# A hybrid decoder layer on one core: which memory the first tiles of the last phase take, and how the final norm is shared out

## The chip, the cores and the metric

The kernel runs on 1 core of a Trainium2 chip. The metric is the device time of one execution in microseconds (us), and the median of several runs stands for a kernel. A core has a matrix engine (PE, whose weight loads are listed as PEld), a vector engine (DVE), a scalar engine (ACT), a general engine (POOL, GpSimd) and a sync engine (SP). Each works through its own list of instructions in order. They meet through semaphores and the on-chip memory (SBUF); matrix products arrive in a separate accumulation memory (PSUM). Transfers are issued from SP, ACT or GpSimd.

## The reference, cut to what matters

One decoder layer over 512 tokens of width 2048: four token mixers side by side, a projection, cross-attention to a memory, and a squared-ReLU MLP of width 8192, with a final RMSNorm. The change lies in the MLP's second half and the norm.

```python
    hn = rmsnorm(h, norm_mlp_g[l])
    h = h + jnp.einsum('blf,fd->bld', jnp.square(jax.nn.relu(jnp.einsum('bld,df->blf', hn, w_up[l]))), w_down[l])
return rmsnorm(h, norm_final_g)
# y = x * rsqrt(mean(x * x) + 1e-6) * g
```

Arithmetic is float32. Every product is made of three matmuls in a reduced format: a value is split into a high part (an ACT copy) and a low part (a DVE subtraction), and high*high, high*low and low*high are added.

## The kernel before

**Phases.** Up to about 799 us come the mixers, the projection and the cross-attention. The up phase (799 to 1494 us) computes the MLP's hidden values in 8 chunks `q` of 4 calls `up_pair(q, pr)`. Each call makes two row blocks by `gemm`, whose weight units go through `wload` (L120 loads 512 KB into `wr`, L125 is the ACT copy `wh`, L126 the DVE difference `wl`). It then squares them, forms seven sums and differences in `z`, splits them into `zh` (L146) and `zl` (L147), and GpSimd stores both to DRAM tensors `ud[q, 0]` and `ud[q, 1]` (L984). The residual goes to DRAM as `xd` tiles. The down phase, from about 1495 us, multiplies the hidden values with `w_down`.

**The down phase.** It is a Strassen-like scheme: a chunk has seven products in place of eight. `down_chunk(q)` loads four blocks of `w_down`: `b22` (1,1), `b11` (0,0), `b12` = (0,1) + (0,0), and `b21` (1,0). A sum of two blocks in memory is made by a second, accumulating load from GpSimd (L1098 with `accum_op`). The products come in the order idx 6, 0, 4, 5, 3, 2, 1; here product 0 is the first, idx 6. Each has its `u` tiles (two DMAs of 512 KB from `ud`, L1026), for some a combination of raw weights on DVE (L1045), four splits of raw weights (L1047 on ACT gives `w2h`, L1048 on DVE gives `w2l`; a ring of five pairs), 48 matmuls (L1057 to L1059) into four PSUM banks, and four evictions into one or two of the accumulators `x1` to `x7` (L1066 the first time on ACT, else L1068 on DVE). `merge` adds accumulators in the last chunks.

**The tail.** In the last chunk, products idx 3 and idx 2 finish the token half `t = 1` (`x7`, `x4`) and the upper columns of `t = 0` (`x3`); idx 1 finishes `x2`. `tail_sums` squares finished tiles on ACT with a row sum, `tail_rs` adds the sums and takes the inverse square root by eleven small DVE operations (`rsqrt`: L161, L162, then three rounds of L166 to L168), and `tail_out` scales a row block by the inverse root and the weight in one DVE operation of 1024 columns (L1170) and stores it from SP (L1173). For `x3`, DVE multiplies by the weight ahead of time (L1132), and ACT scales (L1183).

**Memory and order.** Tiles live in pools, and a pool that is opened after another was closed reuses its memory, each new tile waiting for the old tiles under it. `home` (L998) names the pool of each tile of the down phase: `p2a`, over the residual tiles that are free before the up phase is; `p2x`, over the first half of the activations; `p2w`, over the weight buffers of `wload`; and all others in `p2`, over the second half of the activations and the up phase's `z`, `zh`, `zl`. The order of instructions on an engine is set by a planner, before the run. In its own simulated time it takes, at each moment, the ready instruction of highest priority. Priority is program order, and `urgent()` lifts what is inside it ahead of all that isn't lifted. So an urgent load can go out long before its place in the program, as soon as its memory is free in the planner's view.

Of the kernel before, what the change touches and what calls it, by code (L numbers as in the profile page):

```python
# [13 lines left out]
I32 = mybir.dt.int32  # L14
# [42 lines left out]
def trunk(ctx, tc, A, out):  # L57
# [7 lines left out]
    def pool(name, bufs=1, **kw):  # L65
        return ctx.enter_context(tc.tile_pool(name=name, bufs=bufs, **kw))
# [917 lines left out]
                G.dma_start(ud[q, i][:, :, pr], t.bitcast(F32))  # L984

    NC_ = DFF // P // FC
    for q in range(NC_):
        for pr in range(4):
            up_pair(q, pr)


    zc.close()
    wa.close()
    p2w = pool("down_w", side="left", reuse_waits="tile")
    p2x = pool("down_x", side="left", reuse_waits="tile")
    p2 = pool("down", side="left", reuse_waits="tile")
    acc = {}
# [4 lines left out]
    def slot(name, shape, dt):  # L1002
        return home.get(name, p2).tile(shape, dt, name=name)

    def acc_tile(i):
        t = slot(f"x{i}", [P, 2, 2, L], F32)
# [5 lines left out]
    def flat(t):  # L1012
        return t.rearrange("p a n -> p (a n)")

    us, ws = [0], [0]

    def raw2(n):
        return [slot(f"wq{n}{j}", [P, 4, L], F32) for j in range(2)]

    def u_load(q, idx):  # L1020
        n = us[0] % 3
        us[0] += 1
        uu = []
        for i in range(2):
            t = slot(f"u{n}{i}", [P, 4, 256], F32R)
            Q.dma_start(t.bitcast(F32), ud[q, i][:, idx])  # L1026
            uu.append(t)
        return uu

    def w_tiles():  # L1030
        n = ws[0] % 5
        ws[0] += 1
# [1 line left out]

    sets = [True]

    def down_product(q, idx, w, comb, acc_to, last=None):
        with urgent():
            uu = u_load(q, idx)
# [30 lines left out]
        if last:  # L1070
            for b in range(2):
                for j in range(2):
                    part(j, 0, b)
                    part(j, 1, b)
                    evict(j, b)
                last(b)
# [13 lines left out]

    def down_chunk(q):
        last = q == NC_ - 1
        b22, b11, b12, b21 = (raw2(n) for n in ((0, 1, 2, 3), (1, 2, 0, 3), (2, 0, 1, 3))[q % 3])

        def load(b, i, k, eng=Q, **kw):
            with urgent():
                for j in range(2):
                    eng.dma_start(b[j], A["w_down"][q, i, k, :, j], **kw)  # L1098
# [5 lines left out]
        if not q:  # L1104
# [5 lines left out]
        load(b21, 1, 0)  # L1110
        if q == NC_ - 3:
            merge(2, 2, 1, OP.add)
            merge(6, 6, 1, OP.add)
# [4 lines left out]
        down_product(q, 4, b22, (OP.add, b22, b22, b12), (6,))  # L1118
# [4 lines left out]
        down_product(q, 5, b11, (OP.subtract, b11, b22, b11), (-7, 4) if last else (7,))  # L1123
        load(b22, 1, 0, G, accum_op=OP.add)
        down_product(q, 3, b12, (), (3, 7) if last else (5,))
        if last:
            tail_sums(1, 1, 7)
            tail_sums(0, 1, 3)
            with urgent():
                for b in range(2):  # L1130
                    x = flat(acc[3][:, b])
                    V.tensor_tensor(x, x, fin["g"][:, 1024:], op=OP.mult)  # L1132
# [4 lines left out]
        down_product(q, 2, b22, (), (4,))  # L1137
        if last:
            tail_sums(1, 0, 4)
            tail_rs(slice(2, 4))  # L1140
            with urgent():
                for b in range(2):
                    tail_out(1, b, 1, 7)
                    tail_out(1, b, 0, 4)
        down_product(q, 1, b21, (), (2,), tail if last else None)

    ssq = cp.tile([P, 4, 4], F32, name="sx")
    rf = cp.tile([P, 4], F32, name="rf")
    ss1 = cp.tile([P, 4], F32, name="ss1")
    G.memset(ssq.rearrange("p a b -> p (a b)"), 0.0)  # L1150
    fin = {}

    def tail_sums(t, i, a):
        if not fin:
            g, sq = raw2(NC_ % 3)
            fin["g"], fin["sq"] = flat(g), flat(sq)
            Q.dma_start(fin["g"], A["fin_row"].to_broadcast([P, D]))
        with urgent():
            for b in range(2):
                S.activation(fin["sq"][:, :1024], flat(acc[a][:, b]), AF.Square,  # L1160
                             accum_out=ssq[:, 2 * t + b, i:i + 1])

    def tail_rs(sl):
        with urgent():
            V.reduce_sum(ss1[:, sl], ssq[:, sl], axis=AX.X)
            rsqrt(rf[:, sl], ss1[:, sl], 1.0 / D, EPS)

    def tail_out(t, b, i, a):
        x = flat(acc[a][:, b])
        V.scalar_tensor_tensor(x, x, rf[:, 2 * t + b:2 * t + b + 1], fin["g"][:, 1024 * i:1024 * i + 1024],  # L1170
                               op0=OP.mult, op1=OP.mult)
        r0 = 256 * t + P * b
        Q.dma_start(out[r0:r0 + P, 1024 * i:1024 * i + 1024], x)  # L1173

    def tail(b):
        with urgent():
            for j in range(2):
                S.activation(fin["sq"][:, 1024:1024 + L], acc[2][:, b, j], AF.Square,
                             accum_out=ssq[:, b, 2 * j:2 * j + 1])
            tail_rs(slice(b, b + 1))  # L1180
            tail_out(0, b, 0, 2)
            x = flat(acc[3][:, b])
            S.activation(x, x, AF.Copy, scale=rf[:, b:b + 1])  # L1183
            Q.dma_start(out[P * b:P * b + P, 1024:], x)

    for q in range(NC_):
        down_chunk(q)
# [86 lines left out]
```

## Time and profile before

| | |
|---|---|
| median of 3 runs | 2160.16 us (2156.77 to 2161.19) |
| the profiled execution | 2154.79 us, its span 2152.4 us |
| PE busy | 2088.5 us, 97% of the span |
| DVE, ACT, POOL busy | 1479.9, 907.7, 109.3 us |
| chain that ended last | PE 82%, DVE 7%, DMA 5% |

The span is the time from the first to the last event of the profile; the execution's own time is a little longer. A window row gives, for a stretch of the span, the busy time of each engine and, in brackets, how many instructions that was. The clock is the granted clock of PE as a share of the full one. In a timeline a row gives start, duration, engine, line and operation, with the idle time ahead of it and what ended that in square brackets.

### The profile page before, as it was taken

The page shows a single profiled execution, that of the slowest core. Times are in us where ns is not written, and L with a number is a line of the kernel's source. Part 1 is how long each engine was busy: PE and PEld are TensorE (multiplying, and loading weights), DVE is VectorE, ACT ScalarE, POOL GpSimd, SP SyncE. Part 2 cuts the span into 40 slices and gives each one's busy share as a digit, 9 for nine tenths or more (in the row PEclk, how much of TensorE's full clock was granted, in tenths as well). Part 3 has the DMA queues.
Part 4 walks back from the last instruction along what each step waited for, and adds up shares of the span by engine and source line. Part 5 has one row for each costly group of instructions (what it writes and reads, how often), then busy time and mean ns, then how long its engine had stood idle before and what let it go on. Part 6 is the DMA issues. An engine that isn't in the chain of part 4 may idle for free.

```text
span 2152.4 us, 24931 instructions
## 1 busy us (share of the span) xinstructions
PE 2088.5 (97%) x9340; PEld 1699.7 (79%) x9340; DVE 1479.9 (69%) x2143; ACT 907.7 (42%) x1229; POOL 109.3 (5%) x166
## 2 busy tenths in 40 slices
PE   8999999999999999899999999999699999999997
PEld 6777778777988788688888888888588888888885
DVE  7999999996767663544444444445376777887898
ACT  7565552557434553333233333333343333333334
POOL 0000000100000000100000000000000000000000
PEclk9999999999999999999999999999899999999998
DMA  8553325533433136765655555555879769778872
GB/s 304 169 173 115 116 82 181 164 111 107 143 98 113 40 126 252 254 199 167 197 168 193 167 195 170 188 179 186 298 246 288 253 212 321 233 226 300 250 238 98
DMA packets 111527, 404.83 MB, mean 188 GB/s; under 512 B 13088, under 2 KB 14752, under 8 KB 98992
## 3 DMA queue, kind: packets, MB, share of 16 engines
q1 hardware_dynamic: 89232, 303.64, 41.0%
q0 software_dynamic: 22176, 99.62, 16.5%
q8 instruction: 73, 1.20, 0.2%
q14 instruction: 46, 0.38, 0.1%
HBM read 326.64 MB, written 76.04 MB: 187 GB/s over the span
## 4 chain that ended last, share of the span: by engine, by line
PE 82%; DVE 7%; DMA 5%; issue 2%; ACT 2%; SPq 0%; POOL 0%; ACTq 0%; DVEq 0%; POOLq 0%
PE mm L130 17%; PE mm L132 17%; PE mm L131 16%; PE mm L1058 4%; PE mm L1059 4%; PE mm L1057 4%; PE two L1057 2%; PE two L1058 2%; PE sm L1058 2%; PE sm L1057 2%; PE two L1059 2%; PE sm L1059 2%; DVE wl L126 2%; PE acc L1058 1%; PE acc L1057 1%
## 5 line engine op out<-in xcount | busy, mean ns | idle before, releaser
L132 PE MATMUL mm<-ah,wl 128*128 128x512 f32 (+1 forms) x1920 | 742.9, 387 | 8.3 <-DVE wl L126 8.3
L130 PE MATMUL mm<-ah,wh 128*128 128x512 f32 (+1 forms) x1920 | 743.8, 387 | 5.5 <-ACT wh L125 3.4
L131 PE MATMUL mm<-al,wh 128*128 128x512 f32 (+1 forms) x1920 | 740.2, 385 | 0.0
L125 ACT ACTIVATE wh<-wr 128x1024 fp32r<-128x1024 f32 (+1 forms) x296 | 275.6, 932 | 582.6 <-PE mm L131 450.5
L126 DVE TENSOR_TENSOR wl<-wr,wh 128x1024 fp32r<-128x1024 f32 (+1 forms) x296 | 314.6, 1064 | 182.2 <-ACT wh L125 180.0
L132 PEld LDWEIGHTS mm<-ah,wl 128*128 128x128 f32 x1920 | 361.5, 188 | 84.8 <-DVE wl L126 11.1
L130 PEld LDWEIGHTS mm<-ah,wh 128*128 128x128 f32 x1920 | 361.4, 188 | 82.2 <-ACT wh L125 5.2
L131 PEld LDWEIGHTS mm<-al,wh 128*128 128x128 f32 x1920 | 361.5, 188 | 73.7 <-issue 4.3
L1047 ACT ACTIVATE w2h<-wq 128x1024 fp32r<-128x1024 f32 x224 | 237.6, 1061 | 385.4 <-PE two L1059 106.3
L1048 DVE TENSOR_TENSOR w2l<-wq,w2h 128x1024 fp32r<-128x1024 f32 x224 | 271.1, 1224 | 135.7 <-ACT w2h L1047 135.5
L973 DVE SCALAR_TENSOR_TENSOR r<-mm,rsx 128x512 f32<-128x512 f32 x64 | 44.2, 691 | 165.8 <-PE mm L132 165.0
L1058 PE MATMUL mm<-w2l,u 128*128 128x512 f32 x336 | 132.2, 394 | 0.5 <-DVE w2l L1048 0.5
L1057 PE MATMUL mm<-w2h,u 128*128 128x512 f32 x336 | 131.1, 393 | 1.6 <-ACT w2h L1047 1.6
L1059 PE MATMUL mm<-w2h,u 128*128 128x512 f32 x336 | 132.1, 393 | 0.0
L147 DVE TENSOR_TENSOR zl<-z,zh 128x1792 fp32r<-128x1792 f32 x32 | 64.8, 2026 | 58.4 <-ACT zh L146 50.9
L1057 PE MATMUL two<-w2h,u 128*128 128x512 f32 x224 | 88.5, 396 | 16.9 <-DMA u<-ud 16.9
L1045 DVE TENSOR_TENSOR wq<-wq,wq 128x1024 f32<-128x1024 f32 x64 | 77.7, 1223 | 16.9 <-DMA wq<-in_w_down 16.7
L1058 PE MATMUL two<-w2l,u 128*128 128x512 f32 x224 | 88.5, 395 | 0.0
L1058 PE MATMUL sm<-w2l,u 128*128 128x512 f32 x224 | 88.4, 395 | 0.0
L1057 PE MATMUL sm<-w2h,u 128*128 128x512 f32 x224 | 88.2, 394 | 0.0
L1059 PE MATMUL two<-w2h,u 128*128 128x512 f32 x224 | 87.9, 393 | 0.0
L1059 PE MATMUL sm<-w2h,u 128*128 128x512 f32 x224 | 87.9, 393 | 0.0
(362 smaller groups left out, 2419.3 us busy)
## 6 DMA issues: line engine op xcount, KB each, us to landing
wr<-in_w_up SPq DMA_DIRECT2D x128, 512.0 KB, 3.6
wq<-in_w_down SPq DMA_DIRECT2D x64, 1024.0 KB, 7.8
u<-ud SPq DMA_DIRECT2D x112, 512.0 KB, 6.0
wq<-in_w_down POOLq DMA_DIRECT2D x32, 1024.0 KB, 12.2
wr<-in_w_in SPq DMA_DIRECT2D x56, 512.0 KB, 3.9
ud<-zh POOLq DMA_DIRECT2D x32, 896.0 KB, 4.7
ud<-zl POOLq DMA_DIRECT2D x32, 896.0 KB, 8.1
wr<-in_w_out SPq DMA_DIRECT2D x64, 256.0 KB, 2.9
```

The source lines that it names most:

```text
L125: S.activation(h, r, AF.Copy)
L126: V.tensor_tensor(l, r, h.bitcast(F32), op=OP.subtract)
L130: T.matmul(o, wh, xh, start=start, stop=False)
L131: T.matmul(o, wh, xl, start=False, stop=False)
L132: T.matmul(o, wl, xh, start=False, stop=stop)
L147: V.tensor_tensor(l, src, h.bitcast(F32), op=OP.subtract)
L1045: V.tensor_tensor(flat(r[1]), flat(r[2]), flat(r[3]), op=comb[0])
L1047: S.activation(flat(h), flat(r[0]), AF.Copy)
L1048: V.tensor_tensor(flat(l), flat(r[0]), flat(h).bitcast(F32), op=OP.subtract)
L1057: T.matmul(o[2 * j + b], uh, h[:, p], start=a == 0 and p == 0, stop=False)
L1058: T.matmul(o[2 * j + b], uh, l[:, p], start=False, stop=False)
L1059: T.matmul(o[2 * j + b], ul, h[:, p], start=False, stop=a == 1 and p == 1)
```

## The change

In chunk 0, `b22` and `b11` now are the raw tiles `wq0` and `wq1`, both in the early pool, and their loads and the first `u` load are written into the up loop behind the pairs (1,0), (1,2), (2,0), (2,2) and (3,0). `b12` of chunk 0 takes `wq2`, over the first half of the activations; it is loaded with (0,1), and (0,0) is added by four DVE operations from `b11` and no longer by an accumulating load. The third `u` pair moves from `p2` to the pool over the weight buffers; `wq3` (`b21`) with `x1` and `x6` gets a pool of its own over the second half of the activations; `x7`, `x4`, `x2`, `x5` lie over the old `z`, `zh`, `zl`. In the tail, sums and norms are taken per row block; the inverse root is reached by eight DVE operations after the last square, where it was a sum and eleven; GpSimd multiplies `x7`, `x3` and half of the last blocks by the weight; ACT and DVE share the scalings; and ACT issues half of the stores.

```diff
+    home = {n: "a" for n in ("wq00", "wq01", "wq10", "wq11", "u00", "u01", "w2h0", "w2l0", "w2h1", "w2l1")}
+    home.update({n: "x" for n in ("wq20", "wq21", "u10", "u11", "w2h2", "w2l2")})
+    home.update({n: "w" for n in ("w2h3", "w2l3", "w2h4", "w2l4", "x3", "u20", "u21")})
+    home.update({n: "b" for n in ("wq30", "wq31", "x1", "x6")})
...
+    b22, b11 = raw2(0), raw2(1)
+    early = {(1, 0): lambda: w_load(b22, 0, 1, 1, (0,)), (1, 2): lambda: w_load(b22, 0, 1, 1, (1,)),
+             (2, 0): lambda: w_load(b11, 0, 0, 0, (0,)), (2, 2): lambda: w_load(b11, 0, 0, 0, (1,)),
+             (3, 0): lambda: u_load(0, 6)}
     for q in range(NC_):
         for pr in range(4):
             up_pair(q, pr)
+            if (q, pr) in early:
+                u_first = early[q, pr]()
...
-    home = {n: p2a for n in ("wq00", "wq01", "wq20", "wq21", "u00", "u01", "w2h0", "w2l0", "w2h1", "w2l1")}
-    home.update({n: p2x for n in ("wq10", "wq11", "u10", "u11", "w2h2", "w2l2")})
-    home.update({n: p2w for n in ("w2h3", "w2l3", "w2h4", "w2l4", "x3", "x1")})
...
-        load(b22, 1, 1)
-        load(b12, 0, 1)
-        load(b12, 0, 0, G, accum_op=OP.add)
-        load(b11, 0, 0)
+        if q:
+            w_load(c22, q, 1, 1)
+            w_load(b12, q, 0, 1)
+            w_load(b12, q, 0, 0, eng=G, accum_op=OP.add)
+            w_load(c11, q, 0, 0)
+        else:
+            w_load(b12, q, 0, 1)
+            uu = [u_first, u_load(q, 0)]
             acc_tile(3)
-        down_product(q, 6, b22, (), (3,))
+            uu.append(u_load(q, 4))
+        down_product(q, 6, c22, (), (3,), uu=uu[0])
+        if q:
+            w_load(b21, q, 1, 0)
...
-        down_product(q, 0, b11, (), (2, 6) if q >= NC_ - 3 else (1,))
+        down_product(q, 0, c11, (), (2, 6) if q >= NC_ - 3 else (1,), uu=uu[1])
         if not q:
-            for i in (7, 5, 4, 2):
+            w_load(b21, q, 1, 0)
+            for i in (7, 4, 2, 5):
                 acc_tile(i)
+            with urgent():
+                for j in range(2):
+                    for a in range(2):
+                        x, y = (flat(t[j][:, 2 * a:2 * a + 2]) for t in (b12, c11))
+                        V.tensor_tensor(x, x, y, op=OP.add)
...
+    def gain(x, c0, n):
+        G.tensor_tensor(x, x, fin["g"][:, c0:c0 + n], op=OP.mult)
+
+    def fast_rsqrt(o, h):
...
+        V.tensor_scalar(b, h.bitcast(I32), -0.5, float(0x5F3759DF - (1 << 22) - (1 << 31)), op0=OP.mult, op1=OP.add)
+        yi = b.bitcast(F32)
+        for it in range(3):
+            V.scalar_tensor_tensor(t, yi, h, yi, op0=OP.mult, op1=OP.mult)
+            yo = o if it == 2 else y
+            V.scalar_tensor_tensor(yo, t, 1.5, yi, op0=OP.subtract, op1=OP.mult)
+            yi = yo
...
+    def tail(t, b, lo, hi):
+        with urgent():
+            half_mean(t, b)
+            f = norm(t, b)
+            x, y = flat(acc[lo][:, b]), flat(acc[hi][:, b])
+            S.activation(y, y, AF.Copy, scale=f)
+            put(S, t, b, y, 1024, 1024)
+            V.scalar_tensor_tensor(x, x, f, fin["g"][:, :1024], op0=OP.mult, op1=OP.mult)
+            put(Q, t, b, x, 0, 1024)
+
+    def tail0(b, j):
+        with urgent():
+            x = acc[2][:, b]
+            square(0, b, 1 + 2 * j, x[:, j])
+            if not j:
+                half_mean(0, b)
+                gain(x[:, 0], 0, L)
+                return
+            f = norm(0, b)
+            y = acc[3][:, b]
+            for h in range(2):
+                S.activation(y[:, h], y[:, h], AF.Copy, scale=f)
+                put(S, 0, b, y[:, h], 1024 + h * L, L)
+            V.scalar_tensor_tensor(x[:, 1], x[:, 1], f, fin["g"][:, L:1024], op0=OP.mult, op1=OP.mult)
+            put(Q, 0, b, x[:, 1], L, L)
+            V.tensor_scalar(x[:, 0], x[:, 0], f, None, op0=OP.mult)
+            put(Q, 0, b, x[:, 0], 0, L)
```

## Rows read from the trace of the kernel before

**Rows 1.** Windows of three stretches: busy us and count by engine, clock, DMA.
```profile
799.00:1494.00 695.00, 686.48 (x3049) 568.17 (x3048) 309.57 (x351) 225.90 (x233) 57.26 (x64) 0.99 0.59 194
1494.00:1540.00 46.00, 26.93 (x114) 20.97 (x113) 24.37 (x25) 14.89 (x16) 3.65 (x4) 0.85 0.74 237
1540.00:2100.00 560.00, 560.00 (x2422) 455.96 (x2423) 439.79 (x474) 217.79 (x209) 24.09 (x28) 1.00 0.80 259
```
**Rows 2.** Waits of PE, 790 to 1494 us: total, times, longest.
```profile
PE mm L132 <- DVE wl L126: 6.1, 1, 6.1
```
**Rows 3.** Window in the up phase, columns as in the first group.
```profile
870.00:890.00 20.00, 11.48 (x42) 8.66 (x41) 9.97 (x10) 4.33 (x4) 2.58 (x3) 0.74 0.81 260
```
**Rows 4.** Timeline of DVE, 862 to 886 us.
```profile
870.66 2.36 DVE L1045 TENSOR_TENSOR wq<-wq,wq 128x1024 f32<-128x1024 f32 x2 [2.88 <-DMA wq<-in_w_down]
...
880.15 2.02 DVE L147 TENSOR_TENSOR zl<-z,zh 128x1792 fp32r<-128x1792 f32 x1 [4.57 <-DMA ud<-zl]
```
**Rows 5.** Timeline of POOL, 856 to 892 us.
```profile
857.97 2.05 POOL L1098 DMA_DIRECT2D wq<-in_w_down  x2
863.25 0.94 POOL L984 DMA_DIRECT2D ud<-zl  x1 [3.24 <-DVE zl L147]
```
**Rows 6.** Timeline of the sync queue, 836 to 850 us.
```profile
840.40 2.07 SPq L1098 DMA_DIRECT2D wq<-in_w_down  x4
```
**Rows 7.** Timeline of PE, 1515 to 1546 us.
```profile
1518.95 0.73 PE L1057 MATMUL mm<-w2h,u 128*128 128x512 f32 x2 [1.63 <-ACT w2h L1047]
...
1539.73 0.80 PE L1057 MATMUL two<-w2h,u 128*128 128x512 f32 x1 [16.91 <-DMA u<-ud]
```
**Rows 8.** Windows in the change of phase, columns as in the first group.
```profile
1517.00:1540.00 23.00, 3.93 (x15) 2.37 (x14) 2.51 (x3) 2.60 (x3) 0.89 (x1) 0.70 1.01 295
...
1539.70:1543.70 4.00, 3.97 (x10) 3.18 (x11) 0.00 (x0) 0.00 (x0) 0.00 (x0) 0.54 1.02 411
```
**Rows 9.** Timeline of the sync queue, 1484 to 1540 us.
```profile
1485.61 1.69 SPq L1098 DMA_DIRECT2D wq<-in_w_down  x2
...
1506.01 11.94 SPq L1026 DMA_DIRECT2D u<-ud  x4
...
1518.00 2.56 SPq L1098 DMA_DIRECT2D wq<-in_w_down  x2
1520.92 0.89 SPq L1026 DMA_DIRECT2D u<-ud  x2
```
**Rows 10.** The u loads of L1026, 1505 to 1545 us: landing.
```profile
DMA to landing us min/median/max: 3.6/10.3/18.8
```
**Rows 11.** Timeline of PE, 2135 to 2137 us: the last matmul.
```profile
2136.55 0.39 PE L1059 MATMUL acc<-w2h,u 128*128 128x512 f32 x1
```
**Rows 12.** Timeline of DVE, 2117 to 2153 us.
```profile
2135.49 4.87 DVE L1170 SCALAR_TENSOR_TENSOR x<-x,rf,wq 128x1024 f32<-128x1024 f32 x4
...
2140.35 0.68 DVE L1068 TENSOR_TENSOR x<-x,acc 128x512 f32<-128x512 f32 x1
...
2145.08 0.16 DVE L168 SCALAR_TENSOR_TENSOR rf<-rq_t,rq_y 128x1 f32<-128x1 f32 x1
2145.27 1.28 DVE L1170 SCALAR_TENSOR_TENSOR x<-x,rf,wq 128x1024 f32<-128x1024 f32 x1
```
**Rows 13.** Timeline of ACT, 2135 to 2146 us.
```profile
2141.12 0.63 ACT L1178 ACTIVATE wq<-x 128x512 f32<-128x512 f32 x1 [4.16 <-DVE rq_v L161]
2141.66 0.19 ACT L1178 ACTIVATION_READ_ACCUMULATOR wq<-x 128x1 f32 x1
```
**Rows 14.** Timeline of the sync queue, 2144 to 2153 us.
```profile
2146.45 0.33 SPq L1184 DMA_DIRECT2D out<-x  x1
2146.87 0.53 SPq L1173 DMA_DIRECT2D out<-x  x1
```
**Rows 15.** Groups on POOL: busy us, mean ns of one, idle before.
```profile
L737 POOL MEMSET v<- 128x512 f32 x4 | 1.9, 546 | 0.0
...
masks.py:199 POOL TENSOR_SCALAR_AFFINE_SELECT ident<-ident 128x128 f32<-128x128 f32 x1 | 0.3, 282 | 0.0
```

More of the change, by code (lines that the diff above doesn't have):

```diff
@@ L1013, in flat @@
         return t.rearrange("p a n -> p (a n)")
[L1015 to L1028, printed above, removed]
     def w_tiles():
@@ L1035, in trunk, with down_product @@
     sets = [True]
-    def down_product(q, idx, w, comb, acc_to, last=None):
+    def down_product(q, idx, w, comb, acc_to, last=None, uu=None):
+        if uu is None:
+            uu = u_load(q, idx)
         with urgent():
-            uu = u_load(q, idx)
             wt = {}
@@ L1075, in down_product @@
                     evict(j, b)
-                last(b)
+                    last(b, j)
         else:
@@ L1092, in down_chunk @@
         last = q == NC_ - 1
[L1093 to L1098, printed above, removed]
-        load(b22, 1, 1)
-        load(b12, 0, 1)
-        load(b12, 0, 0, G, accum_op=OP.add)
-        load(b11, 0, 0)
-        if not q:
-            acc_tile(3)
-        down_product(q, 6, b22, (), (3,))
+        w0, w1, w2, b21 = (raw2(n) if q or n > 1 else (b22, b11)[n] for n in range(4))
+        c22, c11, b12 = ((w0, w1, w2), (w1, w2, w0), (w2, w0, w1))[q % 3]
+        uu = [None, None, None]
+        if q:
[6 more added lines that the diff above has]
+            uu = [u_first, u_load(q, 0)]
+            acc_tile(3)
+            uu.append(u_load(q, 4))
+        down_product(q, 6, c22, (), (3,), uu=uu[0])
+        if q:
+            w_load(b21, q, 1, 0)
+        if q == NC_ - 3:
+            merge(2, 2, 1, OP.add)
+            merge(6, 6, 1, OP.add)
         if not q:
@@ L1122, in down_chunk @@
             merge(4, 4, 6, OP.add)
-        down_product(q, 5, b11, (OP.subtract, b11, b22, b11), (-7, 4) if last else (7,))
-        load(b22, 1, 0, G, accum_op=OP.add)
+        down_product(q, 5, c11, (OP.subtract, c11, c22, c11), (-7, 4) if last else (7,))
+        w_load(c22, q, 1, 0, eng=G, accum_op=OP.add)
         down_product(q, 3, b12, (), (3, 7) if last else (5,))
         if last:
-            tail_sums(1, 1, 7)
-            tail_sums(0, 1, 3)
-            with urgent():
+            fin_tiles()
+            for t, a in ((1, 7), (0, 3)):
                 for b in range(2):
-                    x = flat(acc[3][:, b])
-                    V.tensor_tensor(x, x, fin["g"][:, 1024:], op=OP.mult)
+                    square(t, b, 0, flat(acc[a][:, b]))
+                    with urgent():
+                        gain(flat(acc[a][:, b]), 1024, 1024)
         if q == NC_ - 2:
@@ L1136, in down_chunk @@
             merge(3, 3, 5, OP.add)
-        down_product(q, 2, b22, (), (4,))
+        down_product(q, 2, c22, (), (4,))
         if last:
-            tail_sums(1, 0, 4)
-            tail_rs(slice(2, 4))
-            with urgent():
+            for j in range(2):
                 for b in range(2):
-                    tail_out(1, b, 1, 7)
-                    tail_out(1, b, 0, 4)
-        down_product(q, 1, b21, (), (2,), tail if last else None)
+                    square(1, b, 1 + 2 * j, acc[4][:, b, j])
+            for b in range(2):
+                tail(1, b, 4, 7)
@@ L1147, in trunk, with fin_tiles @@
+        down_product(q, 1, b21, (), (2,), tail0 if last else None)
     ssq = cp.tile([P, 4, 4], F32, name="sx")
     rf = cp.tile([P, 4], F32, name="rf")
-    ss1 = cp.tile([P, 4], F32, name="ss1")
+    hv = cp.tile([P, 4], F32, name="ss1")
     G.memset(ssq.rearrange("p a b -> p (a b)"), 0.0)
     fin = {}
[L1153 to L1156, printed above, removed]
+    def fin_tiles():
+        g, sq = raw2(NC_ % 3)
+        fin["g"], fin["sq"] = flat(g), flat(sq)
+        with urgent():
@@ L1157, in tail_sums, with square @@
             Q.dma_start(fin["g"], A["fin_row"].to_broadcast([P, D]))
+    def square(t, b, i, x):
         with urgent():
[L1159 to L1163, printed above, removed]
-        with urgent():
[L1165 to L1173, printed above, removed]
@@ L1175, in tail @@
-    def tail(b):
-        with urgent():
[L1177 to L1184, printed above, removed]
+            S.activation(fin["sq"][:, :x.shape[1]], x, AF.Square, accum_out=ssq[:, 2 * t + b, i:i + 1])
@@ new lines, in half_mean, with norm, put @@
+    def half_mean(t, b):
+        i = 2 * t + b
+        V.reduce_sum(hv[:, i:i + 1], ssq[:, i, :3], axis=AX.X)
+        V.tensor_scalar(hv[:, i:i + 1], hv[:, i:i + 1], 0.5 / D, 0.5 * EPS, op0=OP.mult, op1=OP.add)
+    def norm(t, b):
+        i = 2 * t + b
+        V.scalar_tensor_tensor(hv[:, i:i + 1], ssq[:, i, 3:4], 0.5 / D, hv[:, i:i + 1], op0=OP.mult, op1=OP.add)
+        fast_rsqrt(rf[:, i:i + 1], hv[:, i:i + 1])
+        return rf[:, i:i + 1]
+    def put(eng, t, b, x, c0, n):
+        r0 = 256 * t + P * b
+        eng.dma_start(out[r0:r0 + P, c0:c0 + n], x)
```

36 lines of the change are left out of this document (25 added, 11 removed).

## The prediction

> **What bounds the kernel now.** I read the page first: PE is busy for 97% of the span and is on 82% of the chain that ended last, so only stretches in which PE waits, and the work after its last matmul, can give time back. The windows then show where PE waits [rows 1]. In the up phase (799 to 1494 us) PE is busy for 686.48 of 695 us, in the change of phase (1494 to 1540) for 26.93 of 46, in the down phase (1540 to 2100) for all 560. So there are three places, and the down phase has nothing to give.
>
> The first is the up phase. The list of waits has just two of PE there, 8.5 us together, the longer 6.1 for a split wl [rows 1, 2], and both lie in 870 to 890 [rows 3]. That window has 42 matmuls; the rest of the phase has 3049 - 42 = 3007 in 675 us, or 89 in 20 us [rows 1, 3]. 47 are missing, at 0.2245 us each: 10.6 us, the waits of 8.5 and some 2 us at a lower granted clock (0.74 in the window). The reader should follow the vector queue backwards there. The split that PE waited for stood behind L147, which waited 4.57 us for the store of the zl before it, and behind two sums of w_down tiles (L1045) that waited 2.88 us for their load [rows 4]. That load is the accumulating one: GpSimd issued two of 1 MB at 857.97 and the zl store only behind them at 863.25 [rows 5]; the store was not in before 880.15 [rows 4]. The four plain w_down loads had gone out at 840.40 [rows 6], and PE came through them without a wait.
>
> The second is the change of phase. PE waited 16.91 us until 1539.73 for a u tile, the operand of product idx 4 [rows 7]; the other 2.2 us of the 19.07 idle are waits for splits, the largest 1.63 [rows 1, 7]. By count, 1517 to 1540 has 15 matmuls where the down phase's 4.32 per us would give 99, so 84 are missing, 19.5 us; and 1539.7 to 1543.7, at a granted clock of 0.54, has 10 for 17, another 1.7 [rows 1, 8]. Together 21.2 us. The sync queue tells why: u for idx 4 was issued at 1520.92, behind two loads of b21 and the u tiles of two later products [rows 9], and took 18.8 us to land [rows 10]. Its tile lies in pool "down", over memory that the up phase's last zl still held.
>
> The third is the tail. The last matmul starts at 2136.55 [rows 11] and ends some 0.4 later, but the last eviction starts at 2140.35, behind four scalings L1170 of 4.87 us together [rows 12]. Then come the square at 2141.12 [rows 13], two interleaved norm chains up to 2145.2, a last scaling of 1.28 [rows 12], and the last store, issued at 2146.87 [rows 14], 5.5 us before the span ends at 2152.4.
>
> **The change, part by part.** The sum is made against the profiled execution: 2154.79 us for a span of 2152.4. The median shown, 2160.16, is 5.4 us (0.25%) above it.
>
> *Early loads.* Chunk 0 now fetches b22 and b11 early, both plain, and no longer accumulates (0,0) into b12 early. The plain bytes early stay four loads of 1 MB; both accumulating loads, and the early sums on DVE that waited for them, go. The new places in the program cost or save nothing by themselves: the loads of before stand behind the whole up loop in the program and went out at 840 all the same [rows 6], so the planner fills idle places of the sync queue whatever the emission order. If the new ones bunch at 840 again, that is the burst that PE survived; if they spread, better. Without the accumulating pair the zl store has nothing ahead of it on GpSimd's queue. Gain 10.6, bounds 0 (the burst alone still delays zl or wr) and 10.6.
>
> *Homes.* The memory of b12 and u1 now is the first half of the activations, free when the last product is half done: the same place let loads go at 1485.61 before [rows 9]. u2 goes from pool "down" to old weight buffers, free at the latest with the last up matmul near 1495, where the windows of [rows 1] part. Behind it on the sync queue come two b21 loads and then the u tile of idx 5, which waited until 1506.01 for product 0 to end anyway [rows 9]. Even at the 18.8 us of [rows 10] u2 is in by 1514, before product 2, which two products of 48 matmuls at 0.231 us put at 1517. So the wait of 16.91 goes, and with it the slow clock. What is late next is the vector queue: four additions b12 += b11 are new, and the sums hoisted to 870 [rows 4] come back here, together 6 operations of 1.18 us, 7.1 us. DVE was busy for 24.37 of 46 us in 1494 to 1540 [rows 1], most of it before 1517, and product 2 needs its four splits one by one, 2.8 us apart. I let 1.3 us come through, and the 2.2 us of other waits stay: gain 21.2 - 3.5 = 17.7. Bounds: all 7.1 on the path and 2.2 more, 11.9; nothing, 21.2. The accumulating load into b22 waits for DVE's sums a little longer; its product starts only near 1551.
>
> *Tail.* The two gain multiplications leave DVE for GpSimd, which has nothing else then. Two of the four L1170 become ACT copies, so at most two (2.5 us) can stand ahead of the last eviction. From the last matmul's end (2136.95): eviction 0.68, square with its read-out 0.73 (2141.12 to 2141.85), then one sum and seven steps at 0.19 (the pitch of 2145.08 to 2145.27) [rows 12, 13] make 1.5, to 2139.9. The half rows need two scalings one after the other on ACT with an issue between, 0.63 + 0.33 + 0.63 [rows 13, 14], to 2141.5, where before the last issue stood at 2146.87. Half the bytes in the last store change the 5.5 us behind it little. That is 5.4 us. ACT also has the other half's copies to do at that time; if none of that costs, and if the last store is 0.6 us shorter, 6; with two L1170 in front, 2.9. I take 5.3.
>
> The trace has no GpSimd multiplication. From below, a memset of 128x512 takes 0.546 us, so 1.1 for 1024 columns; from above, the affine select needs 0.282 for 128 columns, so 2.3 [rows 15], or 4.5 if the second input doubles it. I take 2.3, the row that reads and writes. Product idx 3, which ends two products or 22 us before 2137, leaves the tiles ready near 2118. The two on x7 are then done by 2123, those on x3 by 2128, and x3 is read only after 2137: hidden; at 4.5 each the last ends at 2136, still hidden. The Trainium skill (SBUF — State Buffer, Who interferes with whom) says that VectorE and GpSimd share one port pair, as an exclusive lock, when the VectorE operation has two SBUF inputs and the GpSimd one reads SBUF. No row here shows it. By that rule the tail's gain would be lost as the third rival has it.
>
> Sum: 10.6 + 17.7 + 5.3 = 33.6. 2154.8 - 33.6 = 2121.2 for a profiled execution, 2126.6 for the median: **2127 us**.
>
> **Rivals.** *The up stall stays* (something else in the burst at 840 holds zl, or a hoisted split waits for its load): 2137. For it: the stall began only after that burst; against it: the 17 us between 840 and 857.
>
> *The change of phase is bound by the next thing*: DVE's 7.1 us all on the path, or another transfer late. The bytes wanted by product 3 at 1528 (b12, u1, x3, u2, b21, the last ud, u5, x7) are some 11 MB, 38 us at the 295 GB/s of 1517 to 1540 [rows 8] from 1485: just in time. If 7 us come back: 2134; if 10: 2137.
>
> *The gain operations block DVE.* While one runs (2.3 us), a split w2l or an eviction with two SBUF inputs waits. Four times 2.3 are 9 us, less some 3 us by which splits run ahead: 6 us of PE waits in the last two products, so the tail gives nothing: 2133.
>
> *Slower.* The five early loads, now spread, each stop PE as the one at 870 did: the planner puts a split or a chain of ud stores behind a load that lands late, five times 10.6 in place of once. 2160 - 17.7 - 5.3 + 42 = 2179. It decides from about three such stalls on (two added ones, 21 us, still leave a gain). Against it: 1 MB alone is 2.6 us at the 411 GB/s of 1539.7 to 1543.7 [rows 8], and 4 MB at once cost nothing.
>
> *No change*: u2 isn't placed ahead of b21 and the tail rows mix as before, 2157 to 2163.
>
> **How the numbers follow.** The forecast 0.57 (its own range 2121 to 2131); up stall stays 0.14; the next thing in the change of phase 0.13; GpSimd blocks 0.06; no change 0.04; slower 0.06. The predicted time is the forecast's. Low end: all upper bounds, 10.6 + 21.2 + 6 = 38, so 2122, and 4 us for the scatter of the runs: 2118. High end: two of the rivals together, 2127 + 10 + 9, 2146. What is beyond is slower, no change and little more. A measurement of this kernel tells about 0.2% (4.3 us) from no change. Faster by more: 0.90; within: 0.04; slower: 0.06.
>
> **What would show it.** PE without a wait in 799 to 890, and no accumulating load before the down phase. PE's idle time in the change of phase at 2 to 5 us, each for w2h or w2l, none for u; u of idx 4 issued before 1496. Last eviction within 0.1 us of the last matmul's end; 9 to 11 us from there to the end of the span, for 15.5 now. The prediction is wrong if PE waits in the up phase at several places, if a DMA still ends the wait at product 2, or if evictions and splits in the last 20 us stand behind GpSimd.

## The result, and the profile after

The kernel after takes 2125.83 us (median of 4 runs, 2124.01 to 2126.87), the one before 2160.43 beside it (2156.77 to 2161.19): a ratio of 0.9842, 95% interval 0.9825 to 0.9859, so 34.6 us less. The prediction was 2127. That its total comes out so well is luck: two of its three terms are off by about 4 us each, in opposite directions.

The windows of the kernel after, over the stretches of [rows 1, 3, 8] and the end of the down phase (busy us and count of PE, PEld, DVE, ACT and POOL, then the granted clock of PE, the DMA share and GB/s):

```profile
799.00:1494.00 695.00, 695.00 (x3101) 576.27 (x3100) 313.76 (x359) 229.17 (x237) 55.27 (x62) 1.00 0.59 194
870.00:890.00 20.00, 20.00 (x90) 16.52 (x89) 14.19 (x18) 10.76 (x11) 4.46 (x5) 1.00 0.82 287
1494.00:1517.00 23.00, 23.00 (x101) 18.76 (x100) 23.00 (x25) 12.38 (x14) 1.92 (x3) 1.00 0.71 226
1517.00:1540.00 23.00, 23.00 (x101) 18.64 (x100) 13.15 (x11) 11.56 (x13) 1.79 (x2) 1.00 1.02 366
1540.00:2090.00 550.00, 550.00 (x2388) 448.38 (x2387) 446.91 (x487) 212.95 (x203) 24.12 (x28) 1.00 0.80 258
```

PE is busy for every microsecond of the up phase, of the change of phase and of the down phase, at the full granted clock. The list of waits of PE from 780 us to the end is empty. Where 870 to 890 had 42 matmuls [rows 3] it has 90, where 1517 to 1540 had 15 [rows 8] it has 101.

The sync queue of the kernel after, in the up phase and at the change of phase:

```profile
847.19 2.07 SPq L1004 DMA_DIRECT2D wq<-in_w_down  x4
...
1485.02 6.05 SPq L1013 DMA_DIRECT2D u<-ud  x2
1491.12 0.92 SPq L1004 DMA_DIRECT2D wq<-in_w_down  x2
```

The four early loads are written at four places of the up loop and still leave as one burst, as in [rows 6]. The u pair of idx 4, issued at 1520.92 before [rows 9], goes out from 1485.02 on, ahead of b21.

Stages compare kernels better than spans do. Three boundaries can be read in every trace: the first and the last eviction of an up product (L973), the end of the last matmul (its start + 0.39) and the end of the span. The columns below are the differences between them, in us, with the starts read to 0.1; "less" is the median of the kernel before on the same chip minus that of the kernel.

| kernel | up phase | change and down phase | tail | less |
|---|---|---|---|---|
| before | 695.8 | 641.8 | 15.5 | |
| after | 684.8 | 619.8 | 14.0 | 34.6 |
| u2_home | 695.8 | 620.5 | 15.8 | 20.8 |
| u2_back | 684.8 | 643.3 | 13.9 | 13.3 |
| accum_plain | 691.2 | 641.9 | 15.4 | 6.3 |
| no_accum | 688.6 | 641.6 | 15.8 | 7.4 |
| late_emit | 685.2 | 619.8 | 14.0 | 35.1 |
| after_again, after_third | 684.9, 684.8 | 619.8, 619.8 | 14.1, 14.0 | 35.8, 32.4 |
| old_tail | 684.8 | 620.3 | 15.8 | 33.5 |
| gain_dve | 685.2 | 619.7 | 16.3 | 32.8 |
| gain_x7_pool | 685.6 | 619.8 | 12.4 | 36.5 |
| t1_first | 685.5 | 618.7 | 11.9 | 36.3 |

After against before, the stages give 11.0 + 22.0 + 1.4 = 34.4 us (the tail from 15.46 and 14.04), the medians 34.6. The two spans differ by only 27.6, because the profiled execution of before came to its first L973 at 799.3 and that of after at 806.2. PE's instructions up to there stand in the same order, and the medians agree with the stages without that difference, so it is not counted for or against the change (the last section comes back to it).

### The profile page after: what moved, and what is told of

Read it like the earlier page. It is cut to its first block, busy times and chain, and to the rows that moved or that the text cites. A ratio compares the mean times of both kernels' runs of the same rounds, so it can differ in the third digit from the quotient of the medians.

```text
span 2124.8 us, 24968 instructions
## 1 busy us (share of the span) xinstructions
PE 2087.9 (98%) x9340; PEld 1702.2 (80%) x9340; DVE 1486.8 (70%) x2149; ACT 910.3 (43%) x1237; POOL 122.2 (6%) x170
## 3 DMA queue, kind: packets, MB, share of 16 engines
q0 software_dynamic: 21888, 97.53, 16.3%
## 4 chain that ended last, share of the span: by engine, by line
PE 92%; DVE 3%; DMA 2%; ACT 2%; issue 1%; SPq 0%; ACTq 0%; DVEq 0%
PE mm L132 19%; PE mm L130 19%; PE mm L131 19%; PE mm L1072 4%; PE mm L1074 4%; PE mm L1073 4%; PE two L1073 2%; PE two L1072 2%; PE two L1074 2%; PE sm L1074 2%; PE sm L1073 2%; PE sm L1072 2%; PE acc L481 1%; PE acc L1073 1%; PE acc L1074 1%; PE acc L1072 1%
## 5 line engine op out<-in xcount | busy, mean ns | idle before, releaser
L125 ACT ACTIVATE wh<-wr 128x1024 fp32r<-128x1024 f32 (+1 forms) x296 | 275.8, 933 | 591.0 <-PE mm L131 468.5
L973 DVE SCALAR_TENSOR_TENSOR r<-mm,rsx 128x512 f32<-128x512 f32 x64 | 44.2, 691 | 162.9 <-PE mm L132 162.1
L147 DVE TENSOR_TENSOR zl<-z,zh 128x1792 fp32r<-128x1792 f32 x32 | 64.8, 2025 | 55.3 <-ACT zh L146 50.9
L541 DVE SCALAR_TENSOR_TENSOR hc<-pad,wdw,hc 128x512 f32<-128x512 f32 x120 | 85.9, 742 | 0.0
```

The costliest lines, as they stand in the source:

```text
L125: S.activation(h, r, AF.Copy)
L147: V.tensor_tensor(l, src, h.bitcast(F32), op=OP.subtract)
L541: V.scalar_tensor_tensor(hc[c], hps[c][:, o:o + L], w, hc[c], op0=OP.mult, op1=OP.add)
```

## The experiments

**u2_home: one tile's home alone, in the kernel before.**

```diff
-    home.update({n: p2w for n in ("w2h3", "w2l3", "w2h4", "w2l4", "x3", "x1")})
+    home.update({n: p2w for n in ("w2h3", "w2l3", "w2h4", "w2l4", "x3", "u20", "u21")})
```

The tile x1 gives up its place for it and goes to the pool "down".

> The kernel before with one edit: the third u pair takes the place of x1 in the pool over the weight buffers. Theory: the two stalls are separate, each with its own cause. The stall of the up phase stays (8.5 us of PE waits), the 16.9 us wait for u goes with its slow clock: 2160 - 20 = 2140 us, 2137 to 2144, and PE waits of 2 to 4 us for splits in the change of phase. Rival: another late transfer takes the place (the second rival of the prediction): 2146 to 2152, with a PE wait that a DMA ends.

Measured: 2138.89 us (2137.5 to 2141.85), ratio 0.9910 [0.9890, 0.9931]. The waits of PE from 780 us to the end of the down phase (total, times, longest):

```profile
PE mm L132 <- DVE wl L126: 5.3, 2, 5.0
PE mm L130 <- ACT wh L125: 2.6, 1, 2.6
```

Both belong to the up phase. The wait for u and the waits for splits in the change of phase are gone, and that stage is as short as in the kernel after to within 0.7 us. One line of the home table is worth 21 of the 34.6 us, and no other transfer takes the place of the late one.

**u2_back: the reverse, in the kernel after.**

```diff
-    home.update({n: "w" for n in ("w2h3", "w2l3", "w2h4", "w2l4", "x3", "u20", "u21")})
-    home.update({n: "b" for n in ("wq30", "wq31", "x1", "x6")})
+    home.update({n: "w" for n in ("w2h3", "w2l3", "w2h4", "w2l4", "x3", "x1")})
+    home.update({n: "b" for n in ("wq30", "wq31", "x6", "x7")})
...
-            uu.append(u_load(q, 4))
...
+            uu[2] = u_load(q, 4)
```

The second load now stands behind the accumulator tiles of the next products.

> The changed kernel with only the third u pair back over the last zl and loaded behind b21, as before the change; x1 and x7 move places for it. Theory: the up phase runs without a PE wait, the wait for u comes back: some 13 to 17 us of PE wait ended by a DMA in the change of phase, 2141 to 2147 us. Rival: the change's gain there came mostly from the absent accumulating load and not from u's place: a wait under 6 us, 2128 to 2133 us.

Measured: 2146.35 us (2145.33 to 2148.97), ratio 0.9942 [0.9925, 0.9960]. The waits of PE:

```profile
PE two L1072 <- DMA u<-ud: 12.5, 1, 12.5
PE mm L1073 <- DVE w2l L1063: 3.3, 1, 3.3
PE mm L1072 <- ACT w2h L1062: 2.6, 1, 2.6
```

The wait for u comes back, and two waits for splits with it, so the change of phase loses its whole gain while the up phase keeps its own. The two stalls are independent. The sync queue's own list of waits names the memory:

```profile
SPq L1013 <- DMA ud<-zl: 19.3, 1, 19.3
```

Here the load itself waits 19.3 us for the store of the last zl, whose place it takes, and then lands in under 5 us. In the kernel before no such wait is on record: the load stood behind others in the queue [rows 9] and was slow to land [rows 10]. So the same place costs about as much in both kernels, in one by the wait for the store itself, in the other by the order on the queue.

**accum_plain: the accumulating load made a plain one, in the kernel before.**

```diff
-        load(b12, 0, 0, G, accum_op=OP.add)
+        load(b12, 0, 0, G, **({"accum_op": OP.add} if q else {}))
```

> The kernel before, where the second load into b12 of chunk 0 is plain and not accumulating; this leaves out the addition of block (0,1) there. Same place in GpSimd's queue, same bytes from memory, same early sums on the vector engine. Theory A: the up phase stalled since the accumulating transfers themselves are slow and hold the zl store behind them; the 8.5 us of PE waits go: 2149 to 2151 us. Theory B: the queue place or the burst of loads did it, plain or not: the waits stay, 2158 to 2161 us.

Measured: 2153.38 us (2151.49 to 2156.63), ratio 0.9973 [0.9962, 0.9985], between the two forecasts. Waits of PE in the up phase, and two lines of ACT from there:

```profile
PE mm L130 <- ACT wh L125: 2.4, 1, 2.4
PE mm L132 <- DVE wl L126: 1.7, 1, 1.7
...
877.53 0.63 ACT L974 ACTIVATE z<-r 128x512 f32<-128x512 f32 x1 [6.08 <-DVE r L973]
878.07 1.99 ACT L125 ACTIVATE wh<-wr 128x1024 fp32r<-128x1024 f32 x2
```

And the landing of the zl store that GpSimd issued at 865.15, one transfer:

```profile
DMA to landing us min/median/max: 12.3/12.3/12.3
```

The waits halve, from 8.5 [rows 1, 2] to 4.1: the one for a wl falls from 6.1 to 1.7, the one for a wh is 2.4 in both kernels. The store lands after 12.3 us where before it took 16.8 (issued at 863.25, and L147, which waited for it, starts at 880.15 [rows 4, 5]). So the accumulation itself is one part of the stall and not all. The wait for wh is a matter of order: the copy L125 stands on ACT behind L974, which needs the product that PE has just ended.

The store's place on GpSimd's queue does not explain why it was late, for loads on the sync queue were late too. The windows from 864 to 870 of the kernel before and of this one, and the landing of the two wr loads (L120) that the sync queue issued after 864, in the same order:

```profile
864.00:870.00 6.00, 6.00 (x28) 4.88 (x27) 3.59 (x8) 3.49 (x4) 0.33 (x2) 1.00 1.02 221
864.00:870.00 6.00, 6.00 (x27) 4.83 (x27) 5.49 (x9) 3.36 (x6) 0.91 (x1) 1.00 1.02 388
...
DMA to landing us min/median/max: 11.4/11.7/12.0
DMA to landing us min/median/max: 8.0/8.1/8.2
```

The DMA engines are busy all the time in both (share 1.02), but with the accumulating loads under way they move 221 GB/s in place of 388.

**no_accum: that load left out.**

```diff
-        load(b12, 0, 0, G, accum_op=OP.add)
+        if q:
+            load(b12, 0, 0, G, accum_op=OP.add)
```

> The kernel before, with one thing left out: chunk 0's accumulating load of block (0,0) into b12. So chunk 0's b12 is block (0,1) alone (this part of the sum is missing), the early burst is four plain loads, and GpSimd issues nothing but the stores of the activations; the two early sums on VectorE stay. With that load plain instead of accumulating the waits of the up phase were 4.1 us in place of 8.5 and the time 2153.4. Theory A (what was left then is the load itself, its place on GpSimd's queue and its bytes): no wait in the up phase, some 10 us less than before, 2149.5. Theory B (what was left is the two sums on VectorE, 2.4 us, hoisted ahead of the splits): the waits stay at about 4 us, 2153.5.

Measured: 2151.67 us (2148.75 to 2158.71), ratio 0.9966 [0.9953, 0.9978], midway between the two theories. The landing of the same zl store in this kernel, issued at 868.35:

```profile
DMA to landing us min/median/max: 6.8/6.8/6.8
```

Its only wait of PE in the up phase, two operations of VectorE ahead of it, and a window behind it (columns as in the first fence):

```profile
869.25 0.50 PE L132 MATMUL mm<-ah,wl 128*128 128x512 f32 x1 [1.83 <-DVE wl L126]
...
863.17 1.22 DVE L1045 TENSOR_TENSOR wq<-wq,wq 128x1024 f32<-128x1024 f32 x1
...
864.90 1.22 DVE L1045 TENSOR_TENSOR wq<-wq,wq 128x1024 f32<-128x1024 f32 x1
...
870.00:880.00 10.00, 10.00 (x39) 8.13 (x38) 6.90 (x9) 4.62 (x5) 1.79 (x2) 0.84 0.92 310
```

The store now lands after 6.8 us: 16.8, 12.3, 6.8 with two accumulating loads ahead of it, two plain ones, none. (In the kernel after, the like store lands after 6.9.) But one wait of 1.8 us for a wl and a granted clock of 0.84 stay: the two early sums on VectorE now run at 863.17 and 864.90, ahead of the split. In the kernel before they ran at 870.66, later and behind their load [rows 4].

By the up phase's length, the 11.0 us of the stall are 4.6 for the accumulation, 2.6 for the load's presence (with the order that the planner gives the engines because of it), and 3.8 that stay in no_accum. The medians of the two kernels, 1.1 us apart, can't tell the second step from noise; it is read from one profile of each. Neither theory was right alone. The rows point to the two sums for the 3.8, since the early plain loads are four of 1 MB in the kernel after too; no run left the sums out by themselves.

**late_emit: the early loads written behind the whole up loop, in the kernel after.**

```diff
-            if (q, pr) in early:
-                u_first = early[q, pr]()
+    for e in early.values():
+        u_first = e()
```

> The changed kernel with the early loads written behind the whole up loop. Theory: the planner sends them out as soon as their memory is free wherever they stand, in one burst near 845; time as the changed kernel, 2124 to 2128 us, no PE wait in the up phase. Rival: writing them into the loop is what keeps the up phase free of stalls: 4 to 11 us longer, 2130 to 2137 us.

Measured: 2124.53 us (2123.24 to 2127.77), ratio 0.9842 [0.9824, 0.9859], the stages as after. Where the loads are written changes nothing; what they no longer contain does.

**old_tail: the kernel after with the whole tail of before**, beside the kernel after itself (after_again). The diff is the tail's part of the change, reversed.

> The changed kernel with the whole tail of before (norm chain of eleven operations, gains and scalings on the vector engine, all stores from the sync queue). Theory from the trace of the changed kernel: from the end of the last matmul to the end of the span 14.0 us now and 15.5 before, so the new tail is worth only 1.4 us: 2126 to 2129 us. Rival, the prediction's term: 5.3 us, 2130 to 2133 us.

> The changed kernel once more, as the measure for the three runs beside it: 2124 to 2128 us, ratio 0.982 to 0.986.

Measured: 2128.07 us (2125.97 to 2131.21), ratio 0.9846 [0.9826, 0.9866], against 2125.74 (2124.79 to 2129.29), 0.9839 [0.9820, 0.9858]. By the tail's length the new one is worth 1.7 us, by the medians 2.3. That is below what these runs can tell, and far below the 5.3 predicted.

Why, the timelines of the kernel after show. GpSimd's first five multiplications in one row, then the last three of them each in its own, and the sixth:

```profile
2094.02 13.48 POOL L1185 TENSOR_TENSOR x<-x,wq 128x1024 f32<-128x1024 f32 x5 [37.89 <-ACT wq L1182]
...
2100.49 3.40 POOL L1185 TENSOR_TENSOR x<-x,wq 128x1024 f32<-128x1024 f32 x1
2103.84 2.40 POOL L1185 TENSOR_TENSOR x<-x,wq 128x1024 f32<-128x1024 f32 x1
2106.20 1.30 POOL L1185 TENSOR_TENSOR x<-x,wq 128x512 f32<-128x512 f32 x1
...
2113.60 1.26 POOL L1185 TENSOR_TENSOR x<-x,wq 128x512 f32<-128x512 f32 x1 [6.10 <-ACT wq L1182]
```

And VectorE in the same time:

```profile
2094.83 1.27 DVE L1083 TENSOR_TENSOR x<-x,two 128x512 f32<-128x512 f32 x2
2096.03 2.24 DVE L1063 TENSOR_TENSOR w2l<-wq,w2h 128x1024 fp32r<-128x1024 f32 x1
...
2102.57 1.33 DVE L1206 SCALAR_TENSOR_TENSOR ss<-sx,ss 128x1 f32<-128x1 f32 x1
2103.94 0.15 DVE L1191 TENSOR_SCALAR mr_b<-ss 128x1 int32<-128x1 int32 x1
...
2104.60 1.66 DVE L1206 SCALAR_TENSOR_TENSOR ss<-sx,ss 128x1 f32<-128x1 f32 x1
2106.19 1.33 DVE L1194 SCALAR_TENSOR_TENSOR mr_t<-mr_b,ss 128x1 f32<-128x1 f32 x1
...
2107.63 0.21 DVE L1194 SCALAR_TENSOR_TENSOR mr_t<-mr_b,ss 128x1 f32<-128x1 f32 x1
...
2108.74 1.28 DVE L1221 SCALAR_TENSOR_TENSOR x<-x,rf,wq 128x1024 f32<-128x1024 f32 x1
...
2113.32 0.68 DVE L1083 TENSOR_TENSOR x<-x,acc 128x512 f32<-128x512 f32 x1
```

Between 2094.02 and 2107.50, while GpSimd works, a one-column L1206 takes 1.33 and 1.66 us and an L1194 1.33, and a split 2.24. At 2107.63, just behind GpSimd's end, L1194 takes 0.21; splits take 1.22 elsewhere. The three long steps of the norm end at 2103.90, 2106.26 and 2107.52, each within 0.02 us of the end of a GpSimd multiplication (2103.89, 2106.24, 2107.50): each waits until GpSimd's instruction is through. The evictions L1083, whose second input comes from PSUM, and L1191, which has one input, keep their 0.6 and 0.15 us. The Trainium skill (SBUF — State Buffer, Who interferes with whom) says that a VectorE instruction with two inputs in SBUF contends with a GpSimd one that reads SBUF, that one with at most one such input does not (outside the 2-port perf modes), and that the port pair they share is an exclusive lock. These rows agree.

PE did not notice, since splits ran far enough ahead. The norm of the half t = 1 did: its first scaling L1221 starts at 2108.74, two of them stand ahead of the last evictions, and the last one starts at 2113.32, 2.56 us after the last matmul ends. Behind it the sixth multiplication holds up a step of the last chain, an L1196 that takes 0.89 us for 0.15. That row of VectorE, and the end of the kernel on ACT's queue:

```profile
2113.98 0.89 DVE L1196 SCALAR_TENSOR_TENSOR mr_y<-mr_t,mr_b 128x1 f32<-128x1 f32 x1
...
2119.02 0.95 ACTq L1212 DMA_DIRECT2D out<-x  x2
```

The second of this pair is the last store. It is issued at about 2119.6, 8.9 us after the last matmul's end, and the span ends 5.1 us later.

**gain_dve: all multiplications by the weight on VectorE.**

```diff
     def gain(x, c0, n):
-        G.tensor_tensor(x, x, fin["g"][:, c0:c0 + n], op=OP.mult)
+        V.tensor_tensor(x, x, fin["g"][:, c0:c0 + n], op=OP.mult)
...
-                gain(x[:, 0], 0, L)
...
-            V.tensor_scalar(x[:, 0], x[:, 0], f, None, op0=OP.mult)
+            V.scalar_tensor_tensor(x[:, 0], x[:, 0], f, fin["g"][:, :L], op0=OP.mult, op1=OP.mult)
```

> The changed kernel with all multiplications by the norm weight on the vector engine, none on GpSimd; the last half block takes gain and scale in one operation. Theory of the shared port: the long small operations on the vector engine (1.3 to 1.7 us in place of 0.2) and the two long splits (2.2 and 2.5 in place of 1.2) go, t = 1 has its norm some 3 us earlier, and the end comes 1 to 4 us earlier: 2122 to 2125 us. Rival: the vector engine now carries 4.9 us more in the last two products and PE waits for splits: 2127 to 2131 us.

Measured: 2128.79 us (2125.96 to 2133.3), ratio 0.9850 [0.9829, 0.9872]; the tail is 16.3 us, longer than after's. The small operations are all back at 0.14 to 0.22 us, so the blocking is shown to be GpSimd's doing, yet nothing is gained. The time is that of the rival, but not for its reason: PE has no wait. VectorE in this kernel:

```profile
2105.87 0.15 DVE L1196 SCALAR_TENSOR_TENSOR mr_y<-mr_t,mr_b 128x1 f32<-128x1 f32 x1
2108.53 0.69 DVE L1083 TENSOR_TENSOR x<-x,mm 128x512 f32<-128x512 f32 x1 [2.51 <-PE mm L1074]
...
2111.02 1.28 DVE L1221 SCALAR_TENSOR_TENSOR x<-x,rf,wq 128x1024 f32<-128x1024 f32 x1
```

An eviction that has to wait 2.51 us for PE stands in the middle of the norm chain of t = 1, and the first scaling starts at 2111.02, after the last matmul. The first store leaves SP at 2112.33, and the span ends 13.6 us later. In between the transfers run without a gap, at 369 to 406 GB/s from 2114 to 2124. That points to a limit which the prediction had not looked for: the stores.

**gain_x7_pool: GpSimd keeps the two on x7 alone.**

```diff
-                        gain(flat(acc[a][:, b]), 1024, 1024)
+                        gain(flat(acc[a][:, b]), 1024, 1024, G if t else V)
```

The last half block is multiplied as in gain_dve.

> As the run before it, but GpSimd keeps the two multiplications of x7, which are the first. Theory of the shared port: only splits are lengthened, no step of a norm chain; 2122 to 2125 us, as good as all on the vector engine or 1 us better as that engine has 2.4 us less to do. Rival (the port is not what lengthens the steps): they stay long with GpSimd idle, and the time is that of the changed kernel, 2125 to 2127 us.

Measured: 2125.03 us (2121.09 to 2127.75), ratio 0.9830 [0.9809, 0.9851]. The tail is 12.4 us for 14.0; the medians, 0.7 us apart, can't tell that. The steps of the norm are short again (none above 0.22 us), as the theory has it. Windows of the kernel after:

```profile
2114.00:2116.00 2.00, 0.00 (x0) 0.00 (x0) 1.93 (x10) 0.86 (x3) 0.86 (x1) 0.50 1.01 401
2116.00:2118.00 2.00, 0.00 (x0) 0.00 (x0) 1.84 (x7) 1.20 (x2) 0.00 (x0) 0.50 0.33 126
```

And of this kernel:

```profile
2114.00:2116.00 2.00, 0.00 (x0) 0.00 (x0) 2.00 (x11) 1.07 (x2) 0.00 (x0) 0.73 1.02 401
2116.00:2118.00 2.00, 0.00 (x0) 0.00 (x0) 1.89 (x6) 1.36 (x3) 0.00 (x0) 0.50 0.97 365
```

(The output is 512 rows of 2048 fp32, 4.19 MB, 10.5 us at 400 GB/s.) In both kernels the first stores are issued just before the last matmul ends, and the transfers then run at 365 to 408 GB/s wherever they run without a gap. After has a gap in 2116 to 2118 (126 GB/s), between the two halves' stores; here there is none, so this tail is as short as the bytes allow from that start.

**t1_first: the norm of t = 1 ahead of everything that can wait**, beside after_third, the kernel after again.

```diff
-                    with urgent():
-                        gain(flat(acc[a][:, b]), 1024, 1024, G if t else V)
+                    if t:
+                        with urgent():
+                            gain(flat(acc[a][:, b]), 1024, 1024, G)
...
             for b in range(2):
                 tail(1, b, 4, 7)
+            one = cp.tile([P, 1], F32, name="one")
+            with urgent():
+                V.tensor_scalar(one, rf[:, 3:4], 0.0, 1.0, op0=OP.mult, op1=OP.add)
+                for b in range(2):
+                    x = flat(acc[3][:, b])
+                    V.scalar_tensor_tensor(x, x, one, fin["g"][:, 1024:], op0=OP.mult, op1=OP.mult)
```

The factor `one` is 1 and is there so that the planner can't lift these operations ahead of the norm. The diff is against gain_x7_pool; `tail` also has its priority doubled.

> The changed kernel with its tail rearranged: GpSimd keeps only the two multiplications on x7; the two on x3 are one VectorE operation each that also reads the norm factor of the second row half, so they can only stand behind that half's norm chain and scalings instead of ahead of its last evictions. Nothing is left out. Theory (what sets the end is when the first of the 4 MB of stores can go out; in the changed kernel the first goes out at 2110, just before the last matmul ends, and all 4 MB at some 400 GB/s are 10.5 us behind it): the chain of the second half starts near 2102 and is not slowed by GpSimd, its first stores go out near 2106, its 2 MB are in before the first half's stores are issued, and the span ends 10 to 11 us after the last matmul's end (14.0 in the changed kernel, 12.4 with GpSimd on x7 alone): about 2122. Rival (the end is set by the work behind the last matmul alone: eviction, square, chain, scalings, last store): the early stores change nothing, 12 to 12.5 us behind the last matmul as with GpSimd on x7 alone, 2125.

> The changed kernel once more, unaltered, beside the other two on the same chip: 2124 to 2127, with 13.5 to 14.5 us from the last matmul's end to the span's end.

Measured: 2122.75 us (2120.7 to 2123.35), ratio 0.9824 [0.9812, 0.9837], against 2126.68 (2124.88 to 2127.81), 0.9843 [0.9831, 0.9856]. No run of the one reaches a run of the other; the medians differ by 3.9 us. VectorE in t1_first:

```profile
2103.86 1.28 DVE L1228 SCALAR_TENSOR_TENSOR x<-x,rf,wq 128x1024 f32<-128x1024 f32 x1
...
2107.70 2.47 DVE L1172 SCALAR_TENSOR_TENSOR x<-x,one,wq 128x1024 f32<-128x1024 f32 x2
...
2110.16 0.68 DVE L1083 TENSOR_TENSOR x<-x,acc 128x512 f32<-128x512 f32 x1
```

And its windows:

```profile
2108.00:2110.00 2.00, 1.35 (x6) 0.77 (x5) 2.00 (x2) 0.70 (x2) 0.00 (x0) 1.00 1.01 401
2110.00:2112.00 2.00, 0.00 (x0) 0.00 (x0) 1.91 (x13) 0.72 (x2) 0.00 (x0) 0.93 0.63 246
2112.00:2114.00 2.00, 0.00 (x0) 0.00 (x0) 1.97 (x9) 1.33 (x2) 0.00 (x0) 0.50 0.00 0
```

The first scaling starts 5.5 us ahead of the last matmul's end, where the kernel after has 2.0, and half the bytes are out before 2112. But the transfers then stand still until 2114: the tail is 11.9 us, 0.5 less than with the stores back to back, closer to the rival's 12 to 12.5 than to the theory's 10 to 11, although the median is near the theory's 2122. So the stores bind the tail only down to there; next comes the work behind the last matmul, whose last eviction stands 0.8 us late behind the L1172. In this profile 2.1 of the 3.9 us are the tail. The down phase is 1.1 us shorter too, but nearly all of that lies ahead of the last 400 matmuls, where the edit changes nothing; so what is shown for the edit is the 2.1.

## Why the prediction was right, and where it was not

*Up stall, 10.6 predicted, 11.0 measured.* The chain that the prediction followed holds in its links: accumulating loads, late zl store, late DVE queue. It named the accumulating load as the cause; by no_accum that load accounts for 7.2 us, and the rest stays in a kernel that keeps the sums. Its reason, that the store had the loads ahead of it on GpSimd's queue, is not what the runs show: the loads slowed the transfers of both queues (221 GB/s for 388). The bet that the spread is worth nothing by itself was right (late_emit).

*Change of phase, 17.7 predicted, 22.0 measured.* Which tile was late and why is confirmed from both sides (u2_home, u2_back). The failed step is the 3.5 us allowed for waits that would remain: "I let 1.3 us come through, and the 2.2 us of other waits stay". None did. VectorE's new work did come. In the kernel after, two of the four additions, then the split of the change of phase with the least to spare, and the first matmul that reads it:

```profile
1497.61 2.35 DVE L1139 TENSOR_TENSOR wq<-wq,wq 128x1024 f32<-128x1024 f32 x2
...
1507.03 1.22 DVE L1063 TENSOR_TENSOR w2l<-wq,w2h 128x1024 fp32r<-128x1024 f32 x1
...
1513.20 0.39 PE L1073 MATMUL two<-w2l,u 128*128 128x512 f32 x1
```

VectorE is busy for 23.00 of 23 us up to 1517 and for only 13.15 of the next 23. The additions come between splits that already run ahead: each w2l split from 1491 to 1540 ends at least 4.9 us before its first matmul, so PE never sees them. The 2.2 us of waits for splits were no fixed cost either: they vanish with the late u in u2_home, and 5.9 us of them return with it in u2_back. The tiles say why: idx 4 writes `two` and `sm`, but the matmuls at 1518.95 [rows 7] write `mm`. They are 12 of the product behind it, idx 5, which the planner drew forward because u for idx 4 was late, and PE came to their splits too soon.

*Tail, 5.3 predicted, 1.4 measured.* This is the mis-sized term. The step "eviction 0.68" right behind the last matmul failed: two scalings L1221 and the late norm chain put that eviction 2.56 us back, and GpSimd's last multiplication cost the chain behind it another 0.7. The prediction had allowed for two scalings there with 2.9 in place of 5.4, but it costed GpSimd's work at nothing as long as its data were ready in time. The rival about blocking had the right mechanism at the wrong place: it charged PE with 6 us, and PE lost none. So the last store went out 8.9 us behind the last matmul and not 4.6; the 5.5 us behind it held (5.1 measured). Once that chain is shorter a second limit appears that the prediction had not in its sum: 4.19 MB have to leave behind a start at 2110. GpSimd's multiplication takes 3.09 us on average for 1024 columns here (2.40 the shortest), inside the bounds 1.1 to 4.5, above the 2.3 taken.

The sum, 33.6 against 34.4, is thus closer than its parts, by luck: 4.3 us too little in one term and 3.9 too much in another. The rivals that kept a stall did not occur; neither did the slower one, since the loads bunched and PE survived the burst as before.

## What to carry to other kernels

When one queue or one tile is late, look for the memory it waits for: here a tile's home was worth 21 us, and the place in the program where its load stands was worth nothing under a planner that reorders. Work moved to an idle engine is free only if it holds up no other: here VectorE operations with two SBUF inputs waited for GpSimd's, so look first at short ones in a dependent chain. A tail has two limits, the chain behind the last product and the bytes that must leave: start the stores of what is finished first, before shortening the chain.

## What the runs showed of the hardware

An accumulating load slowed what ran beside it, on both queues: with two of 1 MB under way the DMA engines moved 221 GB/s at a full busy share, with two plain ones 388. A zl store issued behind them from GpSimd landed after 16.8 us, behind the plain ones after 12.3, with neither after 6.8; two wr loads on the sync queue landed after 11.4 to 12.0 us beside the accumulating loads and after 8.0 to 8.2 beside the plain ones.

One-column VectorE operations of 0.15 to 0.21 us took up to 1.66 us while GpSimd multiplied, and ended within 0.02 us of a GpSimd instruction's end, so the loss there is a wait for the remainder of one GpSimd instruction and not a slower rate.

Open: the profiled executions of before and of the three kernels made from it reach their first L973 at 799.3 to 802.9 us, all nine made from after at 804.0 to 806.5. The four of the first group took 1.4 to 5.4 us less than the medians of their kernels. With each execution's distance from its median put back, all thirteen lie at 802.3 to 805.8, before at 804.6 and after at 805.1. That fits a scatter between executions in the first 800 us; no run here shows what makes it.
